# Half of the lo parts of the second feed-forward matrix made by accumulating transfers

## The chip, the core and the metric

The kernel runs on one core of one Trainium2 chip. The metric is the device time of one execution in microseconds (us), the median over the runs shown. A core has five engines with an instruction queue each, which run side by side and wait for one another through semaphores: PE (TensorE, the matrix unit), DVE (VectorE), ACT (ScalarE), POOL (GpSimd) and SP (SyncE, used here to issue transfers). Sixteen DMA engines move data between the device memory (HBM) and the on-chip memory (SBUF); PE writes its sums into PSUM banks.

## What is computed

A trunk of two decoder layers over 256 tokens of width 1024. Each layer is a half-step feed-forward block, a mixer (a gated spatial branch and a differential attention branch), and a second feed-forward block, each followed by a layer norm. The feed-forward block is what matters here:

```python
def _swiglu(x, w1, w3, w2):
    return (jax.nn.silu(x @ w1) * (x @ w3)) @ w2
...
for l in range(DEPTH):                                     # DEPTH = 2
    h = _swiglu(x, ffn_w1[l, 0], ffn_w3[l, 0], ffn_w2[l, 0])
    x = _layernorm(ALPHA * x + 0.5 * h, ln_g[l, 0], ln_b[l, 0])
    h = _mixer(x, l, ...)
    x = _layernorm(ALPHA * x + h, ln_g[l, 1], ln_b[l, 1])
    h = _swiglu(x, ffn_w1[l, 1], ffn_w3[l, 1], ffn_w2[l, 1])
    x = _layernorm(ALPHA * x + 0.5 * h, ln_g[l, 2], ln_b[l, 2])
```

All data is float32. `w1` and `w3` are 1024 x 2816, `w2` is 2816 x 1024, and there are four feed-forward blocks in all, so four products with a `w2`.

## The kernel before

Each product is made from split operands. A float32 matrix W is replaced by `hi`, W rounded to the matrix unit's float32r format, and `lo` = W - `hi`, and a product x W becomes three products on PE: x_hi W_hi + x_hi W_lo + x_lo W_hi. So for each weight there are three steps before PE can use it: a transfer brings the raw weights from HBM, ACT copies them to `hi` (which rounds), and DVE subtracts `hi` from the raw weights to give `lo`.

`stream` (from line 147) does this for one tile of 128 x 2048 weights, one MB. It takes a `raw` buffer, issues the load on SP's queue (line 153), and then makes two **pieces** of 128 x 1024: for each, a `hi` buffer and a `lo` buffer, ACT's copy at line 166 and DVE's subtraction at line 168. There are 4 `raw` buffers and 8 `hi` and 8 `lo` buffers, taken in turn. A `raw` buffer is free for the next load when all that reads it is done, and a `hi` or `lo` buffer is free when PE has done its last matmul with the piece that was in it eight pieces earlier. So loads run up to four tiles ahead of the conversion, and the conversion up to eight pieces ahead of PE.

`w2` is consumed by `gemm_b`, called twice in each block, once for each half of the 1024 output columns. One call has 22 row blocks (k) of 128, in five tiles of four and one tile of two, so 11 pieces of two row blocks each; the two calls of a block together have 22, called p0 to p21 below (p0 to p10 in the first call). With a piece, PE makes 12 matmuls of 128 x 512 (line 208: two row blocks, two halves of the tokens `t`, three products); the second of each three is the first to read `lo`. The last pieces of a call are held back and run for t = 0 first and then again for t = 1, so that the first half of the tokens is finished earlier: in the first call these are p9 and p10, in the second, with `tail=14`, p15 to p21.

Before `w2` a block runs `gemm_a2` over `w1` and `w3`. There each call has four pieces, and PE goes over all four `hi` parts first (line 220) and then over all four `lo` parts (line 227), so `hi` buffers come free before `lo` buffers. ACT and DVE also empty the PSUM banks there (lines 228 to 232), apply silu, and split the result. After `w2` comes a layer norm and `gemm_b2` of the next stage, whose first weight tiles go to borrowed buffers (`lhi`, `llo`) and are converted while `w2` is still being multiplied.

PE's order is written out by hand. The order on ACT, DVE, POOL and SP is set by a scheduler that places instructions by a priority counted in steps of the program (`step`), with `behind` holding one back until a named instruction has been issued. Each of these queues runs strictly in order. POOL has little to do: the loads of the norm's two vectors (`bc`, line 383), some small arithmetic, and the second half of the rotary embedding.

Of the kernel before, what the change touches and what calls it, by code (L numbers as in the profile page):

```python
# [15 lines left out]
AF = mybir.ActivationFunctionType  # L16
ALU = mybir.AluOpType
# [9 lines left out]
FT = DFF // P  # L27
# [6 lines left out]
CH = 2048  # L34
HC = CH // 2
# [15 lines left out]
def trunk(ctx, tc, x, xT, w13a, w13b, w2, wb, wqk, wa, wbr, wo, gateb, sgug, sgub, sguwT, sgubias, lam, diffg,  # L51
          lng, lnb, lngT, lnbT, cosT, sinT, out):
    nc = tc.nc
    V, A, G, PE = nc.vector, nc.scalar, nc.gpsimd, nc.tensor
# [15 lines left out]
    def name(s):  # L70
        serial[0] += 1
        return f"{s}_{serial[0]}"

    def bank():
        return psum.tile([P, 512], F32, tag="main", name=name("bank"))
# [29 lines left out]
    def step():  # L105
        chunk[0] += 1
        tc.cur_priority = chunk[0] * STEP
# [33 lines left out]
    latest, added, emptied, silu, turned_by = [None, None], [None], [None], [None], [None]  # L141

    def behind(ins):

        return tc.issue_after(ins) if ins is not None else nullcontext()

    def stream(src, width=CH, sub=HC, lent=(), after=(None, None)):

        step()
        raw = raw_pool.tile([P, CH], F32, tag="raw", name=name("raw"))
        nc.sync.dma_start(raw[:, :width], src)
        out = []
        for o in range(0, width, HC):
            if o // HC in lent:
                hi, lo = ([act.tile([P, 512], F32R, tag="slot", name=name(n)) for _ in range(2)] for n in ("lhi", "llo"))
                at = [(hi[j], lo[j]) for j in range(2)]
            else:
                hi = hi_pool.tile([P, HC], F32R, tag="hi", name=name("whi"))  # L160
                lo = lo_pool.tile([P, HC], F32R, tag="lo", name=name("wlo"))
                at = [(hi[:, p : p + sub], lo[:, p : p + sub]) for p in range(0, HC, sub)]
            for p, (h, w) in zip(range(0, HC, sub), at):
                r = raw[:, o + p : o + p + sub]
                with behind(latest[0]):
                    A.activation(h, r, AF.Copy)  # L166
                with behind(after[o // HC] or latest[1]):
                    V.tensor_tensor(out=w, in0=r, in1=h.bitcast(F32), op=ALU.subtract)  # L168
            out.append((hi, lo))
        return out  # L170
# [39 lines left out]
    def gemm_a2(srcs, xc, zs, rs=lambda: s512("r"), scale=1.0):  # L210

        b, got = [], []
        for src in srcs:
            got += stream(src)
            for hi, _ in got[-2:]:
                b.append(bank())
                for k in range(KT):
                    PE.matmul(b[-1], hi[:, k * P : (k + 1) * P], xc(k), start=k == 0, stop=False)  # L220
                beat(0.65)
        for n, (_, lo) in enumerate(got):
            s = slice(n % 2 * T, (n % 2 + 1) * T)
            if n % 2 == 0:
                r, z = rs(), zs(n // 2)
            for k in range(KT):
                PE.matmul(b[n][:, :T], lo[:, k * P : (k + 1) * P], xc(k)[:, :T], start=False, stop=k == KT - 1)  # L227
            emptied[0] = A.activation(r[:, s], b[n][:, T:], AF.Copy, scale=scale).ins  # L228
            if scale == 1.0:
                a = V.tensor_tensor(out=z[:, s], in0=b[n][:, :T], in1=r[:, s], op=ALU.add)  # L230
            else:
                a = V.scalar_tensor_tensor(out=z[:, s], in0=b[n][:, :T], scalar=scale, in1=r[:, s], op0=ALU.mult,
                                           op1=ALU.add)
            added[0] = a.ins
            beat(0.35)
            if n % 2:
                yield n // 2, z

    def rows_b(ps, t, k0, piece, xh, xl, kts, c0=0, n=512):

        hi, lo = piece
        for j in range(2):
            k, o = k0 + j, j * 512 + c0
            wh, wl = (w[j][:, c0 : c0 + n] if isinstance(w, list) else w[:, o : o + n] for w in (hi, lo))
            three(ps[:, :n], xh(k)[:, t * P : (t + 1) * P], xl(k)[:, t * P : (t + 1) * P], wh, wl,
                  k == 0, k == kts - 1)
        beat(n / 1024)

    def gemm_b(src, kts, xh, xl, done, tail=4, last=()):

        blocks = [[(bank(), c, n) for c, n in (last if t else ()) or ((0, 512),)] for t in range(NT)]
        held = []
        for c in range(0, kts, 4):
            nk = min(4, kts - c)
            for i, piece in enumerate(stream(src[:, c * 512 : (c + nk) * 512], nk * 512)):
                k = c + 2 * i
                if k >= kts - tail:
                    held.append((k, piece))
                    continue
                for t in range(NT):  # L260
                    for ps, o, n in blocks[t]:
                        rows_b(ps, t, k, piece, xh, xl, kts, o, n)
        for t in range(NT):
            for ps, o, n in blocks[t]:
                for k, piece in held:
                    rows_b(ps, t, k, piece, xh, xl, kts, o, n)
                done(t, ps[:, :n], o, n)

    def gemm_b2(srcs, xh, xl, done, norm=None):

        lent, after = [()] * 4, [(None, None)] * 4
        if norm:
            lent = [(0, 1), (0,), (), ()]
            after[1:3] = (None, norm.ends[0]), (norm.ends[0], norm.ends[0])
        ps = [[bank() for _ in range(2)] for _ in range(NT)]
        got = [[None] * 4 for _ in range(2)]
        for t in range(NT):
            for c in range(2):  # L280
                if norm:
                    norm.ready(t, c)
                    after[3] = [norm.xlo.get((0, 1))] * 2
                for m in range(2):
                    n = 2 * c + m
                    if t == 0:
                        got[m][2 * c : 2 * c + 2] = stream(srcs[m][:, c * CH : (c + 1) * CH], sub=512, lent=lent[n],
                                                           after=after[n])
                    for i in range(2 * c, 2 * c + 2):
                        rows_b(ps[t][m], t, 2 * i, got[m][i], xh, xl, KT)  # L290
            with behind(latest[0] if t == 0 else None):
                done(t, ps[t])
# [200 lines left out]
    def ffn(l, f, i, norm, last=False):  # L493
# [26 lines left out]
        for j in range(FB, FT, 2):  # L520
            for m, z in gemm_a2([w13a[l, f, j - FB + m] for m in range(2)], both, lambda m: t512("silu")):
# [4 lines left out]
                if norm is None and j + m == FB:  # L526
                    beside(setup(s[:, :1]), 0)
        ln = Norm(l, i, 2.0 * ALPHA, 4.0 * EPS, s[:, :1], last)
        gemm_b(w2[l, f, 0], FT, hh, hl, lambda t, p, c, n: ln.part(t, 0, p))

        def done(t, p, c, n):
            ln.part(t, 512 + c, p)
            if c + n == 512:
                ln.finish(t, ((2, 1.5), (2, 1))[t])

        gemm_b(w2[l, f, 1], FT, hh, hl, done, tail=14, last=((0, 256), (256, 256)) if last else ())
        return ln.close()

    def mixer(l, i, norm):
# [146 lines left out]
        for h in range(2):  # L686
            def got_v(t, ps, c, n):
                A.activation(vg[t][:, h], ps, AF.Gelu)
                V.bn_stats(out=vst[t][:, h * 6 : h * 6 + 6], in_=vg[t][:, h])
            gemm_b(wb[l, V_, h], KT, xh, xl, got_v)  # L690
# [157 lines left out]
```

## Time and profile before

| What | us |
|---|---|
| median of 3 runs (1243.22 to 1244.21) | 1243.42 |
| profiled execution, first to last instruction (span) | 1242.5 |
| PE busy | 1236.6 (100%) |
| DVE busy | 873.1 (70%) |
| ACT busy | 756.0 (61%) |
| POOL busy | 86.0 (7%) |
| moved by DMA: 241.87 MB | mean 195 GB/s |

The profile is a page of one execution on the chip, taken by the hardware profiler. Its parts are the busy time of each engine, the chain of work that ended last (followed back from the last instruction, at each step to what released it), the groups of instructions by source line with their count, busy time, mean duration and the idle time before them, and the transfers with the time from issue to landing. The trace behind the page can be asked for more: the waits, the timeline of one engine in a stretch, and the busy time of all engines by stretch. A busy PE is not a PE at its peak, because matmuls overlap; gaps in its timeline are what counts. The profiler's span is 0.9 us shorter than the median of the runs.

### The profile page before, as it was taken

How to read it: one execution, taken by the hardware profiler on the slowest of the kernel's cores; microseconds unless marked ns; L12 is line 12 of the kernel's file. 1: busy time of each engine (PE TensorE's matmuls, PEld its weight loads, DVE VectorE, ACT ScalarE, POOL GpSimd, SP SyncE). 2: the span in 40 equal slices, each digit the busy share in tenths (PEclk: the TensorE clock that was granted, in tenths of full speed). 3: DMA queues.
4: the chain of work that ended last, by engine and by line, in shares of the span. 5: the costliest groups of instructions: out<-in, count | busy, mean ns of one | idle time of the engine just before them, and what ended most of it. 6: DMA issues, size and time to landing. Idle time of an engine off the chain costs nothing.

```text
span 1242.5 us, 17870 instructions
## 1 busy us (share of the span) xinstructions
PE 1236.6 (100%) x6703; PEld 1064.1 (86%) x6703; DVE 873.1 (70%) x1532; ACT 756.0 (61%) x1388; POOL 86.0 (7%) x184
## 2 busy tenths in 40 slices
PE   9999999999999999999999999999999999999998
PEld 8888888888888888888888888888888888888887
DVE  6766567876587977665677665679756879766753
ACT  6776446679665566664466664466786555766640
POOL 0100000144100000000000000002430000000000
PEclk9999999999999999999999999999999999999999
DMA  9765645654754745556545546556556456455540
GB/s 352 276 204 183 224 171 187 227 167 165 248 183 145 244 162 205 177 180 253 194 169 191 192 159 250 203 184 206 162 175 228 165 174 233 170 203 203 165 174 35
DMA packets 40679, 241.87 MB, mean 195 GB/s; under 512 B 5344, under 2 KB 6416, under 8 KB 14480
## 3 DMA queue, kind: packets, MB, share of 16 engines
q1 hardware_dynamic: 36624, 227.82, 52.1%
q0 software_dynamic: 3536, 12.13, 3.0%
q8 instruction: 52, 0.85, 0.3%
q10 hardware_dynamic: 432, 0.79, 0.2%
q14 instruction: 35, 0.29, 0.1%
HBM read 235.47 MB, written 1.05 MB: 190 GB/s over the span
## 4 chain that ended last, share of the span: by engine, by line
PE 99%; DVE 0%; ACT 0%; issue 0%; DVEq 0%; ACTq 0%
PE bank L220 38%; PE bank L208 35%; PE bank L227 20%; PE bank L323 2%; PE sbank L588 1%; PE sbank L474 1%; PE sbank L637 1%; PE sbank L718 1%; PE sbank L335 0%; PE sbank L635 0%; PE sbank L659 0%; PE sbank L508 0%; PE sbank L622 0%; PE sbank L627 0%; PE sbank L446 0%; DVE xtok L454 0%
## 5 line engine op out<-in xcount | busy, mean ns | idle before, releaser
L168 DVE TENSOR_TENSOR wlo<-raw,whi 128x1024 fp32r<-128x1024 f32 (+1 forms) x442 | 490.0, 1127 | 223.4 <-PE bank L227 129.3
L166 ACT ACTIVATE whi<-raw 128x1024 fp32r<-128x1024 f32 (+1 forms) x442 | 425.8, 978 | 279.4 <-PE bank L208 135.3
L220 PE MATMUL bank<-x,whi 128*128 128x512 f32 x1792 | 426.5, 392 | 0.0
L220 PEld LDWEIGHTS bank<-x,whi 128*128 128x128 f32 x1792 | 330.7, 188 | 69.0 <-issue 2.6
L227 PE MATMUL bank<-x,wlo 128*128 128x256 f32 x1792 | 229.9, 284 | 0.0
L227 PEld LDWEIGHTS bank<-x,wlo 128*128 128x128 f32 x1792 | 224.2, 191 | 4.8
L208 PE MATMUL bank<-whi,hhi 128*128 128x512 f32 (+1 forms) x374 | 141.3, 378 | 0.0
L208 PE MATMUL bank<-wlo,hhi 128*128 128x512 f32 (+1 forms) x374 | 141.0, 377 | 0.0
L208 PE MATMUL bank<-whi,hlo 128*128 128x512 f32 (+1 forms) x374 | 140.9, 377 | 0.0
L228 ACT ACTIVATE r<-bank 128x256 f32<-128x256 f32 x256 | 96.5, 380 | 66.0 <-PE bank L227 65.7
L208 PE MATMUL bank<-whi,x 128*128 128x512 f32 x328 | 106.6, 394 | 0.0
L208 PEld LDWEIGHTS bank<-whi,hlo 128*128 128x128 f32 x374 | 70.4, 188 | 13.0
L208 PEld LDWEIGHTS bank<-wlo,hhi 128*128 128x128 f32 x374 | 70.4, 188 | 12.7
L208 PEld LDWEIGHTS bank<-whi,hhi 128*128 128x128 f32 x374 | 70.4, 188 | 12.7
L208 PEld LDWEIGHTS bank<-whi,x 128*128 128x128 f32 x328 | 61.6, 188 | 12.7
L208 PE MATMUL bank<-wlo,x 128*128 128x512 f32 x164 | 64.0, 390 | 0.0
L480 ACT ACTIVATE xf<-sbank,ln_b,ln_g 128x128 f32<-128x128 f32 x80 | 30.0, 456 | 40.2 <-PE sbank L474 40.2
L230 DVE TENSOR_TENSOR silu<-bank,r 128x256 f32<-128x256 f32 x144 | 54.2, 418 | 0.2
L383 POOL DMA_DIRECT2D bc<-in_lng x6 | 3.2, 530 | 727.7 <-DVE bc L382 727.7
L415 DVE SCALAR_TENSOR_TENSOR xtok<-xtok,bank 128x512 f32<-128x512 f32 (+1 forms) x25 | 16.6, 663 | 42.2 <-PE bank L208 42.2
L564 POOL TENSOR_TENSOR swap<-swap,sin_t 128x512 f32<-128x512 f32 x16 | 24.3, 1517 | 242.4 <-DMA swap<-z 226.7
L208 PE MATMUL bank<-lhi,x 128*128 128x512 f32 x120 | 39.9, 396 | 0.0
(183 smaller groups left out, 1254.1 us busy)
## 6 DMA issues: line engine op xcount, KB each, us to landing
raw<-in_w13a SPq DMA_DIRECT2D x72, 1024.0 KB, 5.0
raw<-in_w SPq DMA_DIRECT2D x40, 1024.0 KB, 4.9
raw<-in_wa SPq DMA_DIRECT2D x24, 1024.0 KB, 5.5
raw<-in_wb SPq DMA_DIRECT2D x16, 1024.0 KB, 4.9
raw<-in_wqk SPq DMA_DIRECT2D x16, 1024.0 KB, 5.1
raw<-in_wbr SPq DMA_DIRECT2D x16, 1024.0 KB, 4.9
raw<-in_w13b SPq DMA_DIRECT2D x12, 1024.0 KB, 5.0
raw<-in_wo SPq DMA_DIRECT2D x8, 1024.0 KB, 4.9
```

The costliest lines, as they stand in the source:

```text
L166: A.activation(h, r, AF.Copy)
L168: V.tensor_tensor(out=w, in0=r, in1=h.bitcast(F32), op=ALU.subtract)
L208: PE.matmul(ps, xx, w, start=start and n == 0, stop=stop and n == 2)
L220: PE.matmul(b[-1], hi[:, k * P : (k + 1) * P], xc(k), start=k == 0, stop=False)
L227: PE.matmul(b[n][:, :T], lo[:, k * P : (k + 1) * P], xc(k)[:, :T], start=False, stop=k == KT - 1)
L228: emptied[0] = A.activation(r[:, s], b[n][:, T:], AF.Copy, scale=scale).ins
L230: a = V.tensor_tensor(out=z[:, s], in0=b[n][:, :T], in1=r[:, s], op=ALU.add)
L323: PE.matmul(ps[t][m], x[:, j, o + t * P : o + (t + 1) * P], y, start=k0 + j == 0 and o == 0 and y is hi, stop=k0 + j == KT - 1 and y is lo)
L415: V.scalar_tensor_tensor(out=self.y[t][:, s], in0=self.y[t][:, s], scalar=self.scale, in1=ps, op0=ALU.mult, op1=ALU.add)
L474: PE.transpose(b[:, k * P : (k + 1) * P], self.y[t][:, h * 512 + k * P : h * 512 + (k + 1) * P], ident)
L480: A.activation(xf[:, s], b[:, s], AF.Identity, scale=self.gT[:, f], bias=self.bT[:, f])
L564: turned_by[0] = G.tensor_tensor(out=s3, in0=s3, in1=s, op=ALU.mult).ins
```

## The change

In `gemm_b`, when the matrix has 22 row blocks (which only `w2` has), `stream` gets `added=(1,)`: the second piece of each full tile is converted in another way. ACT still makes `hi` from the raw tile. It then makes a second copy of the raw tile with scale -1 into the `lo` buffer, which rounds to -`hi`, and POOL issues a transfer that reads the same raw weights from HBM once more and adds them into the `lo` buffer, giving W - `hi`. DVE has nothing to do for that piece.

```diff
-    def stream(src, width=CH, sub=HC, lent=(), after=(None, None)):
+    def stream(src, width=CH, sub=HC, lent=(), after=(None, None), added=()):
...
                 r = raw[:, o + p : o + p + sub]
                 with behind(latest[0]):
                     A.activation(h, r, AF.Copy)
+                if o // HC in added:
+                    with behind(latest[0]):
+                        A.activation(w, r, AF.Copy, scale=-1.0)
+                    G.dma_start(w, src[:, o + p : o + p + sub], accum_op=ALU.add)
+                    continue
                 with behind(after[o // HC] or latest[1]):
                     V.tensor_tensor(out=w, in0=r, in1=h.bitcast(F32), op=ALU.subtract)
...
-            for i, piece in enumerate(stream(src[:, c * 512 : (c + nk) * 512], nk * 512)):
+            for i, piece in enumerate(stream(src[:, c * 512 : (c + nk) * 512], nk * 512, added=(1,) if kts == FT else ())):
```

The pieces concerned are p1, p3, p5, p7, p9 in the first call of a block and p12, p14, p16, p18, p20 in the second: 10 in a block, 40 in all. The last tile of a call has one piece only and is converted as before. PE's program is the same, except that its first use of such a piece's `lo` waits for a transfer instead of for DVE.

The first place is ACT's queue at the end of the first block's `w2`. In the rows `whi` is a `hi` buffer, `lhi` a borrowed one of the next stage, `wlo` a `lo` buffer, and the first number tells the buffer: `whi_281` and `whi_283` are p17 and p18, `whi_286` and `whi_288` are p19 and p20, `whi_291` is p21, and `raw_319` is the next stage's first tile. Before:

```order
L166 ACTIVATE whi_281_1674<-raw_280_1672 128x1024
L166 ACTIVATE whi_283_1678<-raw_280_1672 128x1024
L166 ACTIVATE lhi_320_1846<-raw_319_1844 128x512
L166 ACTIVATE whi_286_1684<-raw_285_1682 128x1024
L166 ACTIVATE lhi_321_1847<-raw_319_1844 128x512
L166 ACTIVATE lhi_324_1854<-raw_319_1844 128x512
L166 ACTIVATE whi_288_1688<-raw_285_1682 128x1024
L166 ACTIVATE lhi_325_1855<-raw_319_1844 128x512
```

Here the copy of p20 stands behind three of the four copies from the next stage's tile. The same stretch of ACT's queue with the change, where line 169 is the new negated copy and `wlo_284` and `wlo_289` are the `lo` buffers of p18 and p20:

```order
L166 ACTIVATE whi_281_1682<-raw_280_1680 128x1024
L169 ACTIVATE wlo_284_1687<-raw_280_1680 128x1024
L166 ACTIVATE whi_283_1686<-raw_280_1680 128x1024
L166 ACTIVATE lhi_320_1856<-raw_319_1854 128x512
L166 ACTIVATE lhi_321_1857<-raw_319_1854 128x512
L166 ACTIVATE whi_286_1693<-raw_285_1691 128x1024
L166 ACTIVATE lhi_324_1864<-raw_319_1854 128x512
L166 ACTIVATE lhi_325_1865<-raw_319_1854 128x512
L166 ACTIVATE whi_288_1697<-raw_285_1691 128x1024
L169 ACTIVATE wlo_289_1698<-raw_285_1691 128x1024
L166 ACTIVATE lhi_331_1898<-raw_330_1896 128x512
L166 ACTIVATE whi_291_1704<-raw_290_1702 128x1024
```

The negated copy of p18 stands ahead of that piece's `hi`, and that of p20 behind its `hi` and behind all four copies from the next stage's tile.

The second place is POOL's queue over the first block's `w2`. Before, the two loads of the norm's vectors stand alone between the start of the kernel and the rotary embedding (`swap`):

```order
L360 DMA ln_b_142<-in_lnbT 128x48
L360 DMA lam_81_478<-in_lam 128x512
L383 DMA bc_229_1390<-in_lng 128x1024
L383 DMA bc_230_1393<-in_lnb 128x1024
L564 TENSOR_TENSOR swap_368_2102<-swap_368_2102,sin_t_138 128x512
```

With the change the ten accumulating transfers (line 170) stand there, in the order p1, p3, p5, p7, then the two `bc` loads, then p9, p12, p14, p16, p18, p20:

```order
L170 DMA wlo_239_1407<-in_w2 128x1024
L170 DMA wlo_244_1442<-in_w2 128x1024
L170 DMA wlo_249_1477<-in_w2 128x1024
L170 DMA wlo_254_1512<-in_w2 128x1024
L388 DMA bc_229_1390<-in_lng 128x1024
L388 DMA bc_230_1393<-in_lnb 128x1024
L170 DMA wlo_259_1547<-in_w2 128x1024
L170 DMA wlo_269_1606<-in_w2 128x1024
L170 DMA wlo_274_1641<-in_w2 128x1024
L170 DMA wlo_279_1676<-in_w2 128x1024
L170 DMA wlo_284_1687<-in_w2 128x1024
L170 DMA wlo_289_1698<-in_w2 128x1024
```

Nothing else on POOL moved against its neighbours; SP's queue has the same loads in the same order.

## The prediction

> **What bounds the kernel now.** I read the busy times first, then the chain of work that ended last, then PE's waits, then PE's own line through the stage that the change touches.
>
> ```profile
> span 1242.5 us, 17870 instructions
> PE 1236.6 (100%) x6703; PEld 1064.1 (86%) x6703; DVE 873.1 (70%) x1532; ACT 756.0 (61%) x1388; POOL 86.0 (7%) x184
> PE 99%; DVE 0%; ACT 0%; issue 0%; DVEq 0%; ACTq 0%
> PE sbank L335 <- DVE warm L331: 1.0, 1, 1.0
> PE sbank L446 <- ACT minus L444: 0.7, 1, 0.7
> 128.73 57.15 PE bank L208 x252
> ```
>
> The third line is the chain: 99% of it is PE. The next two are all of PE's waits, 1.7 us in the whole execution, one at the start and one at the end. The last is the first block's `w2` on the chain: 252 matmuls in 57.15 us without a break, 0.227 us each. PE is fed everywhere. DVE's 70% and ACT's 61% are averages that say nothing about a gain: whatever leaves DVE, PE waits for none of it. A gain of 2.5 us (0.2%, about what a measurement of this kernel can tell from no change) has no place to come from, unless PE's own rate rises. So the question is whether each `lo` is still there when PE wants it.
>
> **The clock of a `w2` stage.** With 12 matmuls a piece takes 12 x 0.227 = 2.72 us, and a held piece half of that for each t. PE's first matmul here is at 128.57:
>
> ```profile
> 128.57 0.40 PE L208 MATMUL bank<-whi,hhi 128*128 128x512 f32 x1
> 115.73 0.38 ACT L228 ACTIVATE r<-bank 128x256 f32<-128x256 f32 x1 [0.57 <-PE bank L227]
> 126.85 0.38 ACT L228 ACTIVATE r<-bank 128x256 f32<-128x256 f32 x1 [0.57 <-PE bank L227]
> 131.51 1.06 ACT L166 ACTIVATE whi<-raw 128x1024 fp32r<-128x1024 f32 x1 [0.48 <-PE bank L208]
> 134.24 1.06 ACT L166 ACTIVATE whi<-raw 128x1024 fp32r<-128x1024 f32 x1 [1.66 <-PE bank L208]
> 158.72 1.06 ACT L166 ACTIVATE whi<-raw 128x1024 fp32r<-128x1024 f32 x1 [0.30 <-PE bank L208]
> 161.90 0.63 ACT L166 ACTIVATE lhi<-raw 128x512 fp32r<-128x512 f32 x1 [2.12 <-DMA raw<-in_wb]
> 164.42 1.05 ACT L166 ACTIVATE whi<-raw 128x1024 fp32r<-128x1024 f32 x1
> ```
>
> The copies at 131.51 and 134.24 are p8 and p9, each a fifth of a microsecond after PE has done with p0 and p1 (128.57 + 2.72 = 131.29, and 134.01): conversion runs exactly one round of eight buffers ahead. 158.72 is p18, 161.90 the first copy for the next stage, 164.42 is p20. PE wants the `lo` of a piece 0.23 us after it starts on it: p1 at 131.5, p5 at 142.4, and then, with p9 and p10 in halves and p15 to p20 in halves, p18 at 173.7 and p20 at 176.4 (128.57 + 15 x 2.72 + 5 x 1.36 + 0.23).
>
> **What is taken away.** Forty DVE subtractions and nothing else.
>
> ```profile
> L168 DVE TENSOR_TENSOR wlo<-raw,whi x442: 679/1220/2018, 22.2 to 1213.7; 128x1024 fp32r<-128x1024 f32 x121, 128x512 fp32r<-128x512 f32 x27
> L166 ACT ACTIVATE whi<-raw x442: 613/1060/1069, 21.1 to 1212.6; 128x1024 fp32r<-128x1024 f32 x121, 128x512 fp32r<-128x512 f32 x27
> L383 POOL DMA_DIRECT2D bc<-in_lng x6: 527/530/535, 132.4 to 1177.5; - x6
> ```
>
> 40 x 1.22 = 49 us of DVE, all behind PE: worth 0 on the path. **What is added** on ACT: 40 copies of 1.06 us, 42 us, so ACT goes to about 798. In a `w2` stage ACT then has three copies in the 5.44 us of two pieces, 3.2 us, which fits; at the four copies that stand between two bank evacuations of the `gemm_a2` before it (behind 115.73 and 126.85) it pushes the next evacuation by about 1 us. PE takes that bank again 16 matmuls of its next pass later or more, 3.6 us, so nothing is late: 0. On POOL: 40 issues, by the row of plain loads 0.53 us each, 21 us on an engine that is 7% busy. Behind them wait the two `bc` loads, wanted by the norm tens of microseconds later: 0.
>
> **What decides: the time from issue to landing of an accumulating transfer.** The trace has none. First the time there is, for the four pieces with least of it, from the end of the negated copy to PE's need. p1: the copy follows the evacuation at 115.73 (ends 116.1), so it ends at 117.2, and 131.5 is 14.3 us away. p5 likewise: 126.85, 128.3, 142.4: 14.1 us. p18: its copy now stands ahead of its `hi` and ends at 159.8; 173.7 is 13.9 us away. p20: its `hi` at 164.42 ends at 165.5, the copy at 166.5, and 176.4 is **9.9 us** away. The other six have 16 to 18 us. The old subtraction of p20 needed 1.2 us of that room; the margin is large, but a transfer is a large thing to put in it.
>
> ```profile
> DMA to landing us min/median/max: 4.1/5.1/7.9
> DMA to landing us min/median/max: 3.2/5.0/10.1
> bc<-in_lng POOLq DMA_DIRECT2D x6, 512.0 KB, 4.5
> bc<-in_lnb POOLq DMA_DIRECT2D x6, 512.0 KB, 5.7
> raw<-in_w SPq DMA_DIRECT2D x40, 1024.0 KB, 4.9
> raw<-in_w SPq DMA_DIRECT2D x8, 512.0 KB, 3.3
> ```
>
> The first line is line 383, the `bc` loads from POOL: the same 512 KB into the same 128 rows of 4 KB, landing after 4.1 to 7.9 us. The second is line 153, SP's raw loads. Low end: the accumulating transfer brings in the same bytes and must land no sooner than the quickest plain one, 4.1 us. High end: reading what lies in SBUF, adding and writing back could take as long again as the longest plain load, 2 x 7.9 = 15.8 us. Between them: 512 KB more on SP cost 4.9 - 3.3 = 1.6 us, so a transfer that handles its bytes twice is near 5.1 + 1.6 = 6.7, at most 7.9 + 1.6 = 9.5 in traffic. I take 7: under 9.9, so 0 on the path.
>
> At 15.8 us p1 is 1.5 late; p5 has 14.1 + 1.5, 0.2 late; p18 has 13.9, 1.9 late; p20 has 9.9 + 1.9, 4.0 late. Together 7.6 us a block, 30 us in four: 1274. That is the high end of this term.
>
> The Trainium skill prices the second read: "Collectives: The Full Stack", section "The bandwidth ceiling: the fold count and why AG ≠ RS ≠ AR", says that an add in the DMA engines costs nothing as arithmetic but reads two sources, and gives a measured ratio of 1.93 against a copy. No trace here shows an add; by that ratio the 1.6 us for 512 KB would become an estimated 3.1, 6.6 us in all, which hides too. Read alone it speaks against the change only through the traffic that it doubles.
>
> **The traffic.** 40 x 0.524 = 21 MB more come from HBM.
>
> ```profile
> q1 hardware_dynamic: 36624, 227.82, 52.1%
> q0 software_dynamic: 3536, 12.13, 3.0%
> 117.60:128.60 11.00, 11.00 (x66) 9.73 (x65) 7.19 (x13) 7.06 (x12) 0.00 (x0) 1.00 0.42 143
> 128.60:139.50 10.90, 10.90 (x51) 9.01 (x50) 8.30 (x14) 4.74 (x7) 1.06 (x2) 1.00 0.82 282
> 139.50:150.40 10.90, 10.90 (x50) 9.03 (x49) 4.90 (x4) 4.24 (x4) 0.00 (x0) 1.00 0.75 298
> 150.40:161.20 10.80, 10.80 (x49) 8.97 (x48) 6.59 (x7) 4.25 (x4) 0.00 (x0) 1.00 0.44 147
> 161.20:169.40 8.20, 8.20 (x38) 6.76 (x37) 7.39 (x10) 6.22 (x9) 0.00 (x0) 1.00 0.52 166
> 169.40:178.90 9.50, 9.50 (x43) 7.88 (x42) 0.71 (x2) 1.15 (x2) 0.00 (x0) 1.00 0.71 298
> 155.62 0.33 SPq L153 DMA_DIRECT2D raw<-in_wb  x1
> ```
>
> The last two columns of the six stretches are the DMA engines' busy share and GB/s. Weighted by length they sum to 37.5 of 61.3 us, so 23.8 are free. POOL's queue took 3.0% of 1242.5 for 12.13 MB, 3.07 us for a MB, so ten plain transfers of 0.524 MB take 16 us: they fit. Handled twice they take 32, 8 more than is free; loads then slip. Most have four tiles of room, but the last row's has none: issued at 155.62, landed for the copy at 161.90, for which ACT had already waited 2.12 us, and that copy stands ahead of p19 and p20 in ACT's queue. A slip there of one transfer's 1.6 to 3.2 us takes p20's room to 8.3 or 6.7.
>
> **Sum.** DVE 0, ACT 0, POOL 0, `lo` of 36 pieces 0, p20 0 to 0.2 us in each block: 1242.5 + 0 to 0.8 in the span, and with the 0.9 us that the median stands above it 1243.4 to 1244.2. I forecast 1244.
>
> **Rivals.** *(B) p20 alone is late.* Its transfer takes 8 to 10 us and the next stage's load slips, so PE stops for 1 to 4 us at p20 in every block: 4 to 16 us, about 1250. For it: least room of all, traffic at a share of 0.52 and 0.71 around it. It decides from 8.3 us on. *(C) The transfers come one behind the other, slower than they are wanted.* Ten must pass between 117.2 and 176.4, 59.2 us, 5.9 us each. If the add holds the engines for 7 us each, the tenth lands at 117.2 + 70 + 3 (a plain one's fixed part: 5.1 less 1.6, rounded down) = 190, 14 us late; in four blocks 55 us, 1299; at 6.5 us each, 35 us, 1279. Against it: plain bytes need 1.6. For it: the add, its second read and its write-back are in no row, and four times the plain 1.6 would do it. *(D) Faster.* With DVE's 49 us gone, the norm's chain runs sooner and raw tiles come free sooner. Against it: PE waits 1.7 us in all, and the span holds 1242.5 - 1236.6 = 5.9 us without PE, mostly at its two ends. Half of that would be 3 us, 1240.5.
>
> **How the numbers follow.** Forecast 0.42, B 0.28, C 0.25, D 0.05. B and C are slower by over 0.2%, so slower 0.53, same 0.42, faster 0.05; the likeliest single case is still no change, with its own range 1242 to 1246. The range for all takes in D's near edge, B and the high end of the landing time (1274) and C up to 6.6 us each, 1285; left out are C's slower half (0.13) and most of D.
>
> **What would show it.** PE's waits on DMA for `wlo` at line 208: none if I am right, only at the tenth piece of each block under B, at several under C. The chain should stay at 99% PE. Landing of line 170: 6 to 8 us, below 9.9 at p20. DVE near 825 us busy, ACT near 798, HBM reads up by 21 MB. The forecast falls if that landing is above about 10 us, or if the 57.15 us of the first `w2` stretch break up.

## The result

The changed kernel took 1262.11 us, median of 4 runs (1259.55 to 1263.6); the kernel before, on the same chip, 1243.58 us (1243.22 to 1244.21, 4 runs). The ratio is 1.0146 (95% interval 1.0132 to 1.0161): 18.5 us slower. The spans of the two profiled executions, 1259.8 and 1242.5 us, are 17.3 apart. A span is 1.7 us shorter than the time of its own run here (1259.8 for 1261.52), not the 0.9 by which the prediction went; by that the profiled execution before took about 1244.2. From the page of the changed kernel the span, the busy times, POOL's queue and the chain of work that ended last; its line numbers are five higher behind the edit:

```profile
span 1259.8 us, 17989 instructions
PE 1241.2 (99%) x6703; PEld 1065.6 (85%) x6703; DVE 828.8 (66%) x1492; ACT 789.2 (63%) x1428; POOL 122.2 (10%) x224
q0 software_dynamic: 9296, 33.10, 11.2%
HBM read 256.44 MB, written 1.05 MB: 204 GB/s over the span
PE 47%; DMA 4%; ACT 0%; DVE 0%; issue 0%; DVEq 0%; ACTq 0%
```

DVE lost 44 us, ACT gained 33, POOL 36, and HBM reads rose by 21 MB. The chain is no longer PE from end to end: 4% of the span is DMA. (Its shares do not add up to the whole, because the chain could be followed back only to 606.92 us.) PE's waits, and the landing of the new transfers (line 170: in the groups by source line their issue time min/median/max in ns, then the time from issue to landing in us):

```profile
PE bank L213 <- DMA wlo<-in_w: 11.9, 6, 4.1
PEld bank L213 <- DMA wlo<-in_w: 14.4, 6, 4.6
L170 POOL DMA_DIRECT2D wlo<-in_w x40: 848/866/913, 116.8 to 1227.5; - x40
DMA to landing us min/median/max: 6.1/11.0/20.0
```

Six waits, two in each of the first three blocks. PE's own timeline, from the starts of its matmuls, tells which and what they cost. The table is worked out from the trace of the profiled execution; a gap is the start-to-start distance less the usual 0.23 us, and the slower matmuls are what the next 39 matmuls behind the gaps took beyond that distance.

| Block | p9: landing, gap (us) | p20: landing, gap (us) | slower matmuls behind the gaps (us) | `w2` stretch, first to last matmul start, before to after (us) |
|---|---|---|---|---|
| 1 | 18.4, 0.5 | 10.7, 4.3 | 2.4 | 60.1 to 67.4 |
| 2 | 20.0, 2.1 | 10.5, 1.8 | 0.2 | 60.1 to 64.3 |
| 3 | 20.0, 2.1 | 10.6, 2.0 | 1.8 | 60.1 to 66.1 |
| 4 | 13.6, none | 6.1, none | none | 60.7 to 60.7 |

The stretches grew by 7.3 + 4.1 + 6.0 + 0 = 17.4 us, and the span by 17.3: that is where the time went. Late pieces are the last added ones of each call, p9 and p20, and no others: in the first three blocks every other piece landed 3.5 us or more before PE wanted it. p20 in the first block, on ACT, POOL and PE:

```profile
164.76 1.16 ACT L166 ACTIVATE lhi<-raw 128x512 fp32r<-128x512 f32 x2 [4.12 <-DMA raw<-in_wb]
168.76 1.04 ACT L169 ACTIVATE wlo<-raw 128x1024 fp32r<-128x1024 f32 x1
170.09 0.88 POOL L170 DMA_DIRECT2D wlo<-in_w  x1 [9.24 <-ACT wlo L169]
180.85 0.79 PE L213 MATMUL bank<-wlo,hhi 128*128 128x512 f32 x1 [4.13 <-DMA wlo<-in_w]
```

ACT waited 4.12 us for the next stage's load (2.12 before), made p20's negated copy by 169.8, where the prediction had 166.5, and the transfer issued at 170.09 landed 10.7 us later. The same on the chain in the third block, p9's transfer first, then the next stage's load, then p20's:

```profile
761.06 19.69 DMA wlo<-in_w
780.77 9.57 DMA raw<-in_wb
795.70 10.63 DMA wlo<-in_w
```

The DMA engines' share (second to last column) in the first block's `w2`, before and then after:

```profile
128.00:145.00 17.00, 17.00 (x80) 14.17 (x79) 11.35 (x16) 7.05 (x10) 1.06 (x2) 1.00 0.83 308
145.00:160.00 15.00, 15.00 (x68) 12.43 (x67) 7.84 (x8) 6.37 (x6) 0.00 (x0) 1.00 0.51 177
160.00:175.00 15.00, 15.00 (x68) 12.43 (x67) 9.30 (x12) 7.38 (x11) 0.00 (x0) 1.00 0.66 250
```

```profile
128.00:145.00 17.00, 17.00 (x77) 14.09 (x76) 6.58 (x12) 10.04 (x14) 4.55 (x6) 1.00 0.99 315
145.00:160.00 15.00, 14.62 (x64) 11.77 (x64) 5.20 (x6) 8.20 (x9) 1.77 (x3) 1.00 1.05 308
160.00:175.00 15.00, 15.00 (x68) 12.41 (x67) 7.40 (x10) 8.78 (x13) 1.73 (x2) 1.00 0.92 280
```

The engines are full from 128 to 160 us. (A share above 1 means that the recorded times of packets overlap.) Between 128 and 145 the share rises from 0.83 to 0.99 and the bytes hardly, from 308 to 315 GB/s: the added transfers take engine time out of proportion to their bytes.

What one transfer costs the engines: POOL's queue took 11.2% of 1259.8 = 141.1 us, less the 37.3 us of the plain loads from before, over 40 = 2.6 us of all sixteen. The trace's packet records say the same: a 4 KB row takes 327 ns (median) when it is added and 174 ns when it is only written, in the kernel `plain_transfer` below, a factor of 1.88. The Trainium skill ("Collectives: The Full Stack", "The bandwidth ceiling: the fold count and why AG ≠ RS ≠ AR") has 1.93, measured on a ring of collectives: the trace here is near it.

### The profile page after: what moved, and what is told of

Same layout as the page of the kernel before. It is cut to its first block, busy times and chain, and to the rows that moved or that the text cites. A ratio compares the mean times of both kernels' runs of the same rounds, so it can differ in the third digit from the quotient of the medians.

```text
span 1259.8 us, 17989 instructions
## 1 busy us (share of the span) xinstructions
PE 1241.2 (99%) x6703; PEld 1065.6 (85%) x6703; DVE 828.8 (66%) x1492; ACT 789.2 (63%) x1428; POOL 122.2 (10%) x224
## 3 DMA queue, kind: packets, MB, share of 16 engines
q0 software_dynamic: 9296, 33.10, 11.2%
## 4 chain that ended last, share of the span: by engine, by line
PE 47%; DMA 4%; ACT 0%; DVE 0%; issue 0%; DVEq 0%; ACTq 0%
PE bank L225 19%; PE bank L213 16%; PE bank L232 10%; DMA wlo<-in_w 3%; DMA raw<-in_wb 1%; PE sbank L593 1%; PE sbank L479 0%; PE sbank L642 0%; PE sbank L723 0%; ACT wlo L169 0%; ACT lhi L166 0%; PE sbank L640 0%; PE sbank L664 0%; PE sbank L513 0%; PE sbank L627 0%
## 5 line engine op out<-in xcount | busy, mean ns | idle before, releaser
L173 DVE TENSOR_TENSOR wlo<-raw,whi 128x1024 fp32r<-128x1024 f32 (+1 forms) x402 | 441.3, 1116 | 244.1 <-PE bank L232 133.0
L170 POOL DMA_DIRECT2D wlo<-in_w x40 | 34.8, 870 | 629.7 <-ACT silu L528 325.5
L213 PEld LDWEIGHTS bank<-whi,hhi 128*128 128x128 f32 x374 | 71.3, 191 | 13.3
L169 ACT ACTIVATE wlo<-raw 128x1024 fp32r<-128x1024 f32 x40 | 42.2, 1055 | 19.0 <-PE bank L213 18.9
```

The lines of the kernel that those rows point to most:

```text
L169: A.activation(w, r, AF.Copy, scale=-1.0)
L170: G.dma_start(w, src[:, o + p : o + p + sub], accum_op=ALU.add)
L213: PE.matmul(ps, xx, w, start=start and n == 0, stop=stop and n == 2)
```

## The experiments

| Kernel | Transfers | Median, us | Ratio to before, 95% interval |
|---|---|---|---|
| the change | 40 | 1262.11 | 1.0146 (1.0132 to 1.0161) |
| no_transfer | 0 | 1243.54 | 1.0000 (0.9990 to 1.0010) |
| plain_transfer | 40, no add | 1244.84 | 1.0008 (0.9998 to 1.0017) |
| spare_last_tile | 32 | 1244.43 | 1.0006 (0.9997 to 1.0015) |
| only_last_tile | 8 | 1243.73 | 1.0002 (0.9993 to 1.0011) |
| spare_p20 | 36 | 1249.15 | 1.0045 (1.0030 to 1.0060) |
| next_stage_behind | 40 | 1248.47 | 1.0046 (1.0031 to 1.0062) |
| both_halves | 88 | 1354.11 | 1.0890 (1.0873 to 1.0906) |
| from_sbuf | 40 | 1256.81 | 1.0109 (1.0092 to 1.0126) |
| bc_later | 40 | 1265.60 | 1.0178 (1.0163 to 1.0194) |
| bc_later_and_behind | 40 | 1246.61 | 1.0027 (1.0017 to 1.0036) |

All edits are to the changed kernel. The theory (1) was: PE loses time only where a transfer lands later than the room that its piece has, and nowhere else. Its rivals were ACT's added copies (2), the ten transfers of a block queueing whichever they are (3), and two places too tight for any such transfer (4).

### no_transfer: ACT's part alone

```diff
-                    G.dma_start(w, src[:, o + p : o + p + sub], accum_op=ALU.add)
```

> The forty negated copies on ACT stay and the forty transfers are left out, so lo holds -hi in those pieces. Theory 1 (only the landing of the transfers stops PE): 1243 to 1245 us, PE waits for no lo. Theory 2 (ACT's forty more copies and their places ahead of other work cost part of it): over 1248 us, with PE gaps in the w2 stages that follow late hi parts or late bank evacuations.

1243.54 us, the same as before. In the waits of PE only the two of before are left:

```profile
PE sbank L339 <- DVE warm L335: 1.0, 1, 1.0
PE sbank L450 <- ACT minus L448: 0.7, 1, 0.7
```

So 40 subtractions off DVE are worth nothing and 40 copies on ACT cost nothing: theory 2 falls, and so does every hope of a gain from DVE.

### plain_transfer: the add alone

```diff
-                    G.dma_start(w, src[:, o + p : o + p + sub], accum_op=ALU.add)
+                    G.dma_start(w, src[:, o + p : o + p + sub])
```

> The transfers only write the raw weights over the lo buffer, the addition is left out; bytes from HBM, issue places and waits are the same. Theory 1a (the transfer is slow because it also reads the buffer and adds): landing falls from a median of 11.0 to 6 to 8 us, the DMA engines' time for the POOL queue falls from 11.2% to about 8%, PE gaps go, 1243 to 1247 us. Theory 1b (21 MB more traffic beside the loads is enough): landing stays at 9 to 11 us and the time within 3 us of 1262.

```profile
q0 software_dynamic: 9296, 33.10, 7.9%
L170 POOL DMA_DIRECT2D wlo<-in_w x40: 527/527/533, 116.9 to 1210.8; - x40
DMA to landing us min/median/max: 3.8/6.5/12.7
PE bank L213 <- DMA wlo<-in_w: 0.4, 1, 0.4
```

Same packets, same bytes, same places, without the add: 1.5 us of the engines each (7.9% of 1243.2 less 37.3, over 40) in place of 2.6, landing 6.5 in place of 11.0, one wait of 0.4 us, 1244.84. The add is what is slow, not the 21 MB (theory 1a holds, 1b falls). It also takes 0.87 us to issue on POOL against 0.53.

### spare_last_tile and only_last_tile: which pieces

```diff
-... added=(1,) if kts == FT else ())
+... added=(1,) if kts == FT and c < 16 else ())
...
-... added=(1,) if kts == FT else ())
+... added=(1,) if kts == FT and c == 16 else ())
```

The first edit is `spare_last_tile`, without transfers for p9 and p20; the second is `only_last_tile`, with these two alone.

> The last full tile of each call is converted as before, so p9 and p20 have no transfer and 32 transfers are left. Theory 1 (a transfer costs PE only where it lands later than its room, which is p9 and p20): 1243 to 1246 us, no PE gap over 0.6 us. Theory 3 (the ten transfers of a block queue one behind the other and the last ones are late, whichever they are): p18 becomes the last one and late, 1250 us or more.

> Only the last full tile of each call, p9 and p20, has transfers: 8 in all. Theory 1a (traffic of the other transfers makes them late): they land in 6 to 8 us, p9 is never late, p20 is late by at most 1 us a block: 1243 to 1248 us. Theory 4 (these two places are too tight even for a transfer that has the DMA engines nearly to itself): landing near 11 us, p20 late in three blocks, 1250 us or more.

The landing of line 170 in the two kernels:

```profile
DMA to landing us min/median/max: 8.2/9.3/12.8
DMA to landing us min/median/max: 5.6/10.1/12.1
```

The 32 transfers without p9 and p20 land after 9.3 us in the median, PE waits for none, and the time is 1244.43. p18, the last one then, is not late: theory 3 falls for this number of transfers. The eight at p9 and p20 alone land after 10.1 us, and here the expectation was wrong: 6 to 8 us were expected. p20 takes 9.6 to 9.8 us in the first three blocks even with no other transfer in its queue; in the fourth, which has no next stage to load, it takes 5.6. So the next stage's raw loads beside it are the likely reason, though no run took them away alone. But in the first block p20 is issued at 166.6 instead of 170.1, and in the three blocks it lands 0.2 to 0.3 us before PE wants it. No gap is seen: 1243.73. The landing is as long as theory 4 had it, and still PE loses nothing.

### spare_p20 and next_stage_behind: p9's share and p20's

```diff
-... added=(1,) if kts == FT else ())
+... added=(1,) if kts == FT and (c < 16 or tail < 14) else ())
```

That is `spare_p20`; `next_stage_behind` is:

```diff
-                with behind(latest[0]):
+                with behind(negated[0] if lent else latest[0]):
                     A.activation(h, r, AF.Copy)
...
-                        A.activation(w, r, AF.Copy, scale=-1.0)
+                        negated[0] = A.activation(w, r, AF.Copy, scale=-1.0).ins
```

> Only p20 is converted as before; p9 keeps its transfer, 36 in all. Theory 1 (each late piece has its own price): p9's stalls of 0.5, 2.1 and 2.1 us in the first three blocks stay and p20's (4.3, 1.8, 2.0 us and the slow matmuls behind two of them) go: 1247 to 1251 us. Theory 5 (p9's stall matters only because it shifts p20's): 1243 to 1245 us.

> All forty transfers stay; on ACT the first copies of the next stage's borrowed buffers are held until p20's negated copy has been issued, so p20 no longer waits for the next stage's load. Theory 1 (p20's room of 9.9 us is cut to about 7 us by that load): p20's transfer is issued about 3 us earlier in the first three blocks, its stall falls to at most 1 us; with p9's stalls left the time is 1247 to 1253 us. Theory 4 (the landing alone is too long wherever the copy stands): p20's stall changes by less than 1 us, 1258 us or more.

Without p20's transfer p9's gaps stay, 0.3, 1.7 and 1.9 us, and 1249.15 is measured, 5.5 us above before. 4.3 of them are in the first three `w2` stretches, so p9 has a price of its own (theory 5 falls). With all 40 and the next stage's copies held behind p20's, ACT and POOL in the first block read:

```profile
163.78 1.06 ACT L170 ACTIVATE wlo<-raw 128x1024 fp32r<-128x1024 f32 x1 [1.43 <-PE bank L214]
164.75 1.04 ACT L167 ACTIVATE whi<-raw 128x1024 fp32r<-128x1024 f32 x1
165.69 1.14 ACT L167 ACTIVATE lhi<-raw 128x512 fp32r<-128x512 f32 x2
165.13 0.87 POOL L171 DMA_DIRECT2D wlo<-in_w  x1 [4.56 <-ACT wlo L170]
```

p20's transfer goes out at 165.13, 5 us earlier, and is never late; p9's gaps stay and the time is 1248.47. So p20's lateness was the next stage's load ahead of it on ACT's queue together with a landing of about 10 us, as theory 1 has it.

### both_halves: where the engines are the limit

```diff
-... added=(1,) if kts == FT else ())
+... added=(0, 1) if kts == FT else ())
```

> Every piece of a full tile gets its lo by a transfer, 80 in all. By the 2.6 us of all 16 engines that one transfer took (11.2% of 1259.8 us less the 37 us of the plain POOL loads, over 40) and 2.84 us per MB of loads, a block then needs 20 x 2.6 + 33 = 85 us of the DMA engines in a stretch of about 62 us. Theory 3 (the DMA engines' time is the limit once it is exceeded): 15 to 25 us more in each block, 1300 to 1345 us. Theory 1 alone (landing against room, no shared limit): landing stays near 11 us and the time below 1285 us.

```profile
DMA to landing us min/median/max: 5.5/20.3/30.3
PE bank L213 <- DMA wlo<-in_w: 74.4, 41, 6.7
```

1354.11 us, slower than expected; the expectation had overlooked that the one-piece tiles are added too, 88 transfers and 22 in a block. With 22 the sum is 22 x 2.6 + 33 = 90 us of the engines, and the `w2` stretches of the first three blocks took 91.1, 90.9 and 90.8 us. The agreement is closer than such a sum can promise: the engines' share over these stretches is 0.93, 1.03 or more from 128 to 200 us in the first block and far less behind that; and the fourth block, which has no next stage to load, took 78.4. But full engines for most of the stretch are what theory 3 says: here the engines' time is the limit. With ten transfers in a block they are full for about half of it, and PE stops at two pieces only.

### from_sbuf: the second read

```diff
-                    G.dma_start(w, src[:, o + p : o + p + sub], accum_op=ALU.add)
+                    G.dma_start(w, r, accum_op=ALU.add)
```

> The transfer adds the raw weights out of the raw tile in SBUF in place of reading them from HBM once more; the raw buffer is then held until the transfer has landed. Theory H (reading HBM is what is slow): landing falls to 6 to 8 us, POOL's queue takes under 8% of the engines' time, 1243 to 1250 us. Theory E (the engines' own handling of two streams is what is slow): landing and the queue's share (11.2%) stay within a tenth, 1255 us or more, and later loads on top.

```profile
q0 software_dynamic: 9296, 33.10, 11.8%
DMA to landing us min/median/max: 4.4/6.2/13.6
PE bank L213 <- DMA wlo<-raw: 7.4, 3, 3.5
```

The engines' time did not fall (11.8%), so their own handling of two streams is the cost (theory E). The landing did fall, to 6.2 us, which theory E did not expect. Two things changed at once: the source is nearer, and the loads of the next tiles, waiting for the raw buffers, no longer run beside the transfers. How much is which stays open; the quickest transfers of both kernels, 4.4 and 6.1 us, are 1.7 apart, which is an estimate of the first alone. The 1256.81 us come from p20 in the first three blocks (gaps of 3.8, 1.6 and 2.6 us), issued late, at 174.95 in the first, because the loads are: SP's loads waited 213.0 us in all for these transfers, and ACT 6.4 and 3.8 us for the two loads ahead of that copy.

### bc_later and bc_later_and_behind: p9's place on POOL's queue

```diff
-    def bc_load(src, after):
+    def bc_load(src, after, ins=None):
...
-        G.dma_start(t, src.partition_broadcast(P))
+        with behind(ins):
+            G.dma_start(t, src.partition_broadcast(P))
...
         gemm_b(w2[l, f, 0], FT, hh, hl, lambda t, p, c, n: ln.part(t, 0, p))
+        if not last:
+            ln.g, ln.b = ln.load(summed[0])
```

`summed[0]` is the transfer made last, here p9's, and `ln.load` makes the two `bc` loads; so in the first three blocks they come behind the first call and p9. `bc_later_and_behind` has this edit and that of `next_stage_behind`.

> In the first three blocks the two bc loads stand on POOL's queue behind p9's transfer in place of ahead of it; nothing else moves. Theory 6 (p9 lands after 18 to 20 us because its rows stand in POOL's rings behind two plain loads of 512 KB, about 1.6 us of the engines each and twice that while the raw loads take every other turn): p9 lands after 13 to 15 us, its stalls of 0.5 to 2.1 us go, p20's stay: 1254 to 1259 us. Theory 7 (p9 is late because the engines are full in that stretch, whatever the order): p9 still lands after 17 us or more and the time is within 2 us of 1262.

> As bc_later, and the next stage's first copies are held behind p20's negated copy. All forty transfers stay. If p9's place on POOL's queue and p20's on ACT's are the whole loss: no PE gap over 0.6 us and 1243 to 1245 us, no better than before since PE had nothing to win. If a third place is late once these two are mended: 1247 us or more.

POOL's queue in the first block of `bc_later`, with p9's transfer first:

```profile
134.49 0.87 POOL L171 DMA_DIRECT2D wlo<-in_w  x1 [4.10 <-ACT wlo L170]
135.03 0.89 POOL L390 DMA_DIRECT2D bc<-in_lng  x1
135.57 0.89 POOL L390 DMA_DIRECT2D bc<-in_lnb  x1
```

With the two `bc` loads behind it p9 lands after 12.0, 14.3 and 13.2 us (18.4, 20.0, 20.0 before the edit) and PE does not wait for it, as theory 6 has it. And the kernel is slower, 1265.60, where 1254 to 1259 was expected. p20's gaps grew to 5.0, 3.7 and 3.6 us. The first block's p20, and PE's waits:

```profile
169.82 0.88 POOL L171 DMA_DIRECT2D wlo<-in_w  x1 [9.97 <-ACT wlo L170]
180.51 0.79 PE L214 MATMUL bank<-wlo,hhi 128*128 128x512 f32 x1 [4.80 <-DMA wlo<-in_w]
PE bank L214 <- DMA wlo<-in_w: 11.7, 3, 4.8
```

PE gets to p20 earlier, since p9 no longer holds it up, but p20's transfer is issued no earlier, because it hangs on the next stage's load. The stop has moved, and it is now long enough in all three blocks for 2.5 to 2.8 us of slow matmuls behind it, where the change had 2.3 and 1.7 us of that in two. The two places are not additive: 1.0178 with one mended, 1.0046 with the other, 1.0027 with both. With both, p9 is never late and p20's gaps are 0.4, 2.2 and 0.9 us, its landing 11.5 to 13.3, where it was 8.2 to 9.9 in `next_stage_behind`. (These are of the profiled execution, 1250.65 us, where the median is 1246.61.) That median lies between the two cases of the expectation, nearer to the one with a third place: what is left is p20's longer landing, and why it is longer was not tested. Forty accumulating transfers do not fit without loss in any order tried, and the kernel before stays the fastest: PE has no wait there that a transfer could save.

## Why the prediction was right and where it was wrong

The range (1241 to 1285) held, and "slower" was the likelier sign (0.53). The forecast time, 1244, was that of the case "all hidden", 0.42, and that case did not happen. Both of its signs of falling came: a landing above 10 us, and a first `w2` stretch that breaks up. What came was rival B, p20 late in the blocks that have a next stage to load, with p9 beside it, at 18.5 us instead of 4 to 16. That 1262 lies inside the range is in part luck: B as priced ends near 1260, and the room above it was there for a landing of 15.8 us at every piece and for rival C, and neither came.

*PE has nothing to win; DVE, ACT and POOL cost nothing.* Shown: `no_transfer` at a ratio of 1.0000. DVE near 825 and ACT near 798 were 828.8 and 789.2.

*Room of each piece.* Right for nearly all: p1 and p5, with some 14 us of room, took their 8.4 to 10.5 us unseen, and `spare_last_tile` shows no wait. p20's 9.9 us held where its copy was not delayed (`only_last_tile`: 10.0 from issue to need). The cut by the slipping load, put at 1.6 to 3.2 us, was 3.8 in the first block: the copy ended 41.8 us behind the block's first matmul instead of 37.9.

*Landing of an accumulating transfer, "I take 7".* **This is the step that failed**, by its size. It measured 11.0 in the median. Alone it was right: 5.5 to 6.1 us where no load ran beside it, against the 6.7 of the working. In traffic 9.5 was allowed for at most; p20 took 10.5 to 10.7 in the first three blocks, and the high end of 15.8 was passed by p9's 20.0. "`lo` of 36 pieces 0, p20 0 to 0.2 us" in the sum was 17.4 us.

*The traffic.* The sum had the right size and side: 32 us of engine time in a block by the doubling (26 measured) against 23.8 free. The conclusion from it was not followed through. The working let the loads slip and kept the transfers' own landing as it was, though both share the same full engines; with engine time missing, the transfers could be expected to slip as well.

*p9, among "the other six" with 16 to 18 us.* Its 18 us were right and did not help. POOL's order in the part on the change shows the two `bc` loads just ahead of p9; they were counted as work waiting behind the transfers ("wanted tens of microseconds later: 0"), not as work that p9 waits behind. `bc_later` shows that this place cost 6 us of p9's landing.

*The price of a stop.* Not in the prediction: behind two of the six stops the matmuls ran at half speed for some 4 us each, which made 4.0 of the 17.4 us.

*Rival C* (transfers one behind the other) was not the cause here but is real: `both_halves`. *D* (faster) found nothing, as its argument against had it.

## What to carry to other kernels

A transfer that adds costs the DMA engines nearly twice a plain one (2.6 us against 1.5 here); before moving arithmetic there, sum the engines' time over the stretch, not over the kernel, and if it comes near full, lengthen the transfer's own landing and not only that of its neighbours. Read the queue in both directions: who waits behind the new instruction, and what the new one stands behind. And where the bound engine has no wait, as PE here, taking work off another engine has nothing to win and much to lose. Two late places behind one another hide each other: here, mending the first alone made the kernel slower.

## What the runs showed of the hardware

Behind p20's stop in the first block PE ran at half its clock for some 4.5 us. The granted clock (third column from the end) and the matmul starts after p20's gap in the first block of the changed kernel:

```profile
181.00:184.00 3.00, 3.00 (x7) 2.33 (x8) 0.00 (x0) 0.00 (x0) 0.00 (x0) 0.50 0.10 41
184.00:187.00 3.00, 3.00 (x11) 2.43 (x10) 1.13 (x2) 0.00 (x0) 0.00 (x0) 0.74 0.00 0
187.00:190.00 3.00, 3.00 (x15) 2.45 (x14) 2.65 (x11) 2.35 (x5) 0.00 (x0) 1.00 0.00 0
```

About ten matmuls start 0.43 us apart instead of 0.227. Such a stretch, of 8 to 13 slow matmuls, followed each of the five start-to-start gaps of 3.8 to 5.2 us in the changed kernel, `from_sbuf` and `bc_later`, and, of the seven between 2.0 and 2.9 us in those, `spare_p20` and `bc_later_and_behind`, two (2.3 and 2.4 us) but not the longest (2.9). (`both_halves`, whose gaps stand close together, is left out.) The Trainium skill, "TensorE: Matmul & The Clock Gate", section "Part 1: The HAM clock gate (the "warmup" mystery)", describes such a gate, with an idle window of about 3.4 us and 426.7 ns per cold matmul of 512 columns; the 0.43 us agree, and the two short gaps show that less than 3.4 us can be enough.
